# Gathered expert rows transposed as f32r, with a comparison against fp32 transposes for the first expert

## The chip, the cores and the metric

The kernel runs on one core of one Trainium2 chip. The metric is the device time of one execution, in microseconds (us). The core's engines are TensorE (PE in the profile, with PEld for its weight loads), VectorE (DVE), ScalarE (ACT), GpSimd (POOL) and SyncE (SP), which issues most of the DMAs. Each engine works through a queue of its own in order; semaphores tie the queues together.

## The reference

Two blocks of a model run one after the other on x of 1024 tokens by 1024 features. The first block is a mixer (attention with latent queries and keys, and a chunked recurrent branch) followed by a mixture of experts; the second is two layers of a mixer with four branches. The change lies in the mixture of experts. Each of the 16 experts takes the 128 tokens that have the highest affinity to it:

```python
def ec_moe(x, w_router, w_e_gate, w_e_up, w_e_down):
    B, T, D = x.shape
    cap = CAP_FACTOR * T // N_EXPERTS                  # 128
    aff = jax.nn.softmax((x @ w_router).astype(jnp.float32), axis=-1)
    g, idx = lax.top_k(aff.transpose(0, 2, 1), cap)
    xs = jax.vmap(lambda xb, ib: xb[ib])(x, idx)
    a = jnp.einsum('becd,edf->becf', xs, w_e_gate)
    u = jnp.einsum('becd,edf->becf', xs, w_e_up)
    y = jnp.einsum('becf,efd->becd', jax.nn.silu(a) * u, w_e_down) * g[..., None].astype(x.dtype)
    return jax.vmap(lambda yb, ib: jnp.zeros((T, D), x.dtype).at[ib.reshape(-1)].add(yb.reshape(-1, D)))(y, idx)
```

All of it is fp32; one expert has three weight matrices of 1024 by 1024.

## The kernel before

A product in fp32 accuracy is made of three passes over operands of type f32r (a 32-bit type with fewer bits of mantissa): each operand is split into a high half H, which ScalarE writes by a copy that rounds to f32r (L141), and a low half L, which VectorE makes as the difference (L142). The passes are H by H, L by H and H by L.

The expert stage begins near 1480 us and goes to 2096 us of the span. For expert e:

- `slots(e)` finds the 128 token numbers. VectorE makes eight one-hot tiles `hot` (L1197, 16 buffers), TensorE multiplies each by `pick` and sums into a PSUM tile named "tp" (L1198; each of the eight products is two instructions, 16 in all), and VectorE copies the result to `idxT` (L1199) and to `gsl` (L1200), which holds the gate weights g.
- `tokens(e)` gathers the rows from DRAM with an indirect DMA that POOL issues (L1207), into `xs`, two buffers deep.
- `transposed(xs, "xT")` turns the rows: two times four transposes of 128x128 on TensorE against an identity (L1162), each four into one PSUM tile "tp", which is then split into xTH and xTL. There are two "tp" buffers, shared by `slots`, by the transposes of the rows and by those of the hidden activations ("eT").
- `product(xT, w)` loads the weights in four tiles of 1 MB (twelve tiles deep in all, named ewr and ahead), splits them into ewH and ewL of 128x1024, four buffers of each, and for each of eight k makes six multiplications of 128x512 into `acc` (L1188): ewH by xTH and ewH by xTL for the two halves of the columns, then ewL by xTH.
- The gate product goes through Silu on ScalarE to `ea` (L1212), VectorE multiplies the up product into it (L1231), the result is transposed ("eT") and goes through the down product; VectorE scales it by `gsl[:, e]` (L1237), and POOL adds the rows to the output with a scattering DMA (L1238).

The loop is written so that the transposes for expert e + 1 and the slots of expert e + 2 stand ahead of the up product of expert e. That isn't the order on the chip: a scheduler orders each engine's instructions when the program is built, by its own estimate of the times, so a change at one place can shift instructions elsewhere. The two layers of the second block follow the expert stage; the attention jobs in them (one head by 256 queries each, 20 in the first layer, four of them short, and 16 in the second) are ordered in the same way. `ident` is an fp32 identity, `identr` (L153) the same in f32r, which other transposes use already (L838).

Of the kernel before, what the change touches and what calls it, by code (L numbers as in the profile page):

```python
# [10 lines left out]
F32 = mybir.dt.float32  # L11
F32R = mybir.dt.float32r
U32 = mybir.dt.uint32
I32 = mybir.dt.int32
AF = mybir.ActivationFunctionType
OP = mybir.AluOpType
AX = mybir.AxisListType
# [3 lines left out]
P = 128  # L21
D = 1024
# [100 lines left out]
def build(ctx, tc, A, out):  # L123
# [6 lines left out]
    V, S, G, PE, SY = nc.vector, nc.scalar, nc.gpsimd, nc.tensor, nc.sync  # L130
# [21 lines left out]
    ident = load(const, A["k_ident"], [P, P], "ident")  # L152
    identr = const.tile([P, P], F32R, name="identr")  # L153
# [250 lines left out]
    with ExitStack() as es:  # L404
# [4 lines left out]
        for j in range(4):  # L409
# [3 lines left out]
                               op0=OP.add, op1=OP.mult)  # L413
    with ExitStack() as es:
# [4 lines left out]
        ps = es.enter_context(tile_pool(name="ps1", bufs=1, space=PSUM))  # L419
# [36 lines left out]
        with ExitStack() as es2:  # L456
            tp = es2.enter_context(tile_pool(name="gw", bufs=1, side="right", reuse_waits="tile"))
            bd = block_diagonals(tp, load(tp, A["k_blk"], [P, P], "blk"))
            wg = load(tp, A["w_gate"][0].rearrange("(f p) g -> p f g", p=P), [P, 24, 16], "wg")
            for f in range(8):  # L460
                pt = ps.tile([P, 512], F32, name="gw", bufs=1)
# [15 lines left out]
        for f2 in range(4):  # L477
            wt = wstream(wp, win, 704 + 256 * f2)
            for f in (2 * f2, 2 * f2 + 1):
# [13 lines left out]
                for a, b in ((0, C), (C, N)):  # L493
                    for j in (0, 1, 3, 4):
# [3 lines left out]
                                               op0=OP.mult, op1=OP.add)  # L498
# [75 lines left out]
    with ExitStack() as es:  # L574
        gp = es.enter_context(tile_pool(name="mg", bufs=1, reuse_waits="tile"))
        ps = es.enter_context(tile_pool(name="ps2", bufs=1, space=PSUM))
# [48 lines left out]
        for d, st_ in ((0, 1), (1, -1)):  # L625
            r = DIR[d]
            V.tensor_tensor_scan(Bc[r, ::st_], ones[r, ::st_], LF[r, ::st_], 0.0, op0=OP.mult, op1=OP.add)
        V.tensor_sub(Aa, IG, Bc)
        for d, st_ in ((0, 1), (1, -1)):
            r = DIR[d]  # L630
# [6 lines left out]
        pr = psc()  # L637
# [4 lines left out]
        for h in range(4):  # L642
            f0, b0 = 10 * h, 64 + 10 * h
            V.tensor_tensor_scan(R[:, 2, f0:f0 + 10], R[:, 0, f0:f0 + 10], R[:, 1, f0:f0 + 10], 0.0,
                                 op0=OP.max, op1=OP.add)
# [27 lines left out]
        pt = psc()  # L673
# [475 lines left out]
    with ExitStack() as es:  # L1149
# [6 lines left out]
        def transposed(src, nm):  # L1156
            H = tp.tile([P, 8, P], F32R, name=nm + "H")
            L = tp.tile([P, 8, P], F32R, name=nm + "L")
            for hb in range(2):
                pt = ps.tile([P, 512], F32, name="tp", tag="tp", bufs=2)  # L1160
                for j in range(4):
                    PE.transpose(pt[:, j * P:(j + 1) * P], src[:, (4 * hb + j) * P:(4 * hb + j + 1) * P], ident)  # L1162
                hs_ = slice(4 * hb, 4 * hb + 4)
                split(H[:, hs_].rearrange("p a b -> p (a b)"), L[:, hs_].rearrange("p a b -> p (a b)"), pt)
            return H, L
# [37 lines left out]
        at = lambda e: bass.IndirectOffsetOnAxis(ap=idxT[:, e:e + 1], axis=0)  # L1203

        def tokens(e):
            xs = sp.tile([P, D], F32, name="xs")
            G.indirect_dma_start(out=xs, out_offset=None, in_=h2_scr, in_offset=at(e))  # L1207
            return xs

        def gated(xT, e):  # L1210
# [6 lines left out]
        xs = tokens(0)  # L1217
        slots(1)
        xT = transposed(xs, "xT")
        xs = tokens(1)  # L1220
        with tc.issue_after(chosen.ins):
            a = gated(xT, 0)
# [513 lines left out]
```

## Time and profile before

| | before |
|---|---|
| median of 3 runs | 3334.95 us (3334.73 to 3339.39) |
| the profiled execution | 3336.31 us |
| its span | 3334.5 us |
| mean granted TensorE clock over the span | 0.972 |
| TensorE busy | 3142.5 us, 94% |
| VectorE busy | 2239.7 us, 67% |
| ScalarE busy | 1551.2 us, 47% |
| GpSimd busy | 662.8 us, 20% |

The profile is of one execution, the one with the span in the table. Its views are a page (busy times, slices, the costliest groups), tables by stretch of time, a list of what an engine waited for, and the timeline of one engine. A row of a timeline gives the start, the duration, engine, line and operation, the tiles (out, then in), the shapes, the number of instructions taken together, and in brackets the idle time before and what ended it. In every view a multiplication's record begins when it enters the pipeline, and its end is modelled, so records of TensorE overlap; the distance from one start to the next is what it costs. A granted clock of 1.00 is 2.4 GHz and one of 0.50 is 1.2 GHz.

### The profile page before, as it was taken

What the parts mean: (1) busy time and instruction counts of PE and PEld (TensorE: products, weight loads), DVE (VectorE), ACT (ScalarE), POOL (GpSimd) and SP (SyncE); (2) the same over time, 40 slices, a digit from 0 to 9 for tenths busy, and PEclk for the clock granted to TensorE, in tenths of its full rate; (3) what the DMA queues carried; (4) which work ended last, traced back from release to release, by engine and by line L of the source; (5) the groups of instructions that cost most, each with busy time, mean ns of one, the idle gap of its engine ahead of it and who ended that gap; (6) DMA issues with size and microseconds to landing.
All of it is one profiled execution on the core that took longest, in us unless ns stands there. A gap on an engine that the chain in (4) does not pass through costs nothing. (4 is left out here: it accounts for less than half of the span.)

```text
span 3334.5 us, 48219 instructions
## 1 busy us (share of the span) xinstructions
PE 3142.5 (94%) x17297; PEld 2650.8 (79%) x17297; DVE 2239.7 (67%) x4868; ACT 1551.2 (47%) x3076; POOL 662.8 (20%) x840
## 2 busy tenths in 40 slices
PE   7997998999999999969999999799999998999999
PEld 5885886999998888857888877698877887887787
DVE  4485778767666654498999888777527745642783
ACT  4223444555555222217777767621126824312780
POOL 0012232222222000331121100210114601101450
PEclk9998999999999999979999999899999999999999
DMA  8541112000003532458999998433210033111002
GB/s 295 147 124 36 36 43 65 5 15 10 5 11 104 153 112 64 169 201 319 380 367 386 366 336 303 149 100 108 67 39 32 1 128 127 51 48 50 32 27 101
DMA packets 224011, 425.95 MB, mean 128 GB/s; under 512 B 28684, under 2 KB 121468, under 8 KB 223772
## 3 DMA queue, kind: packets, MB, share of 16 engines
q1 hardware_dynamic: 215708, 393.51, 33.5%
q0 software_dynamic: 8064, 29.36, 3.0%
q8 instruction: 136, 2.23, 0.3%
q14 instruction: 103, 0.84, 0.1%
HBM read 379.22 MB, written 43.61 MB: 127 GB/s over the span
## 5 line engine op out<-in xcount | busy, mean ns | idle before, releaser
L145 PE MATMUL acc<-hH,wHL 128*128 128x512 f32 (+1 forms) x1296 | 485.4, 376 | 5.5 <-ACT wHL L141 3.9
L146 PE MATMUL acc<-hL,wHL 128*128 128x512 f32 (+1 forms) x1296 | 484.1, 374 | 0.0
L147 PE MATMUL acc<-hH,wHL 128*128 128x512 f32 (+1 forms) x1296 | 482.4, 373 | 0.0
L142 DVE TENSOR_TENSOR ewL<-ewr,ewH 128x1024 fp32r<-128x1024 f32 x320 | 377.9, 1220 | 37.1 <-ACT ewH L141 27.7
L141 ACT ACTIVATE ewH<-ewr 128x1024 fp32r<-128x1024 f32 x320 | 335.9, 1061 | 121.9 <-PE acc L1188 116.0
L145 PEld LDWEIGHTS acc<-hH,wHL 128*128 128x128 f32 x1296 | 244.5, 189 | 53.9 <-ACT wHL L141 6.7
L146 PEld LDWEIGHTS acc<-hL,wHL 128*128 128x128 f32 x1296 | 244.6, 189 | 44.5 <-issue 2.6
L147 PEld LDWEIGHTS acc<-hH,wHL 128*128 128x128 f32 x1296 | 244.2, 189 | 44.4 <-issue 1.6
L142 DVE TENSOR_TENSOR wHL<-wr,wHL 128x512 fp32r<-128x512 f32 (+1 forms) x160 | 111.8, 703 | 222.9 <-ACT wHL L141 222.5
L142 DVE TENSOR_TENSOR et<-t,et 128x512 fp32r<-128x512 f32 x264 | 179.6, 685 | 58.6 <-ACT et L141 57.1
L141 ACT ACTIVATE et<-t 128x512 fp32r<-128x512 f32 x264 | 156.3, 605 | 133.6 <-PE t L904 111.7
L141 ACT ACTIVATE wHL<-wr 128x512 fp32r<-128x512 f32 (+1 forms) x160 | 101.8, 639 | 247.5 <-PE acc L146 221.1
L1188 PE MATMUL acc<-ewH,xTL 128*128 128x512 f32 x512 | 203.5, 397 | 2.3 <-DVE xTL L142 2.3
L1188 PE MATMUL acc<-ewH,xTH 128*128 128x512 f32 x512 | 204.4, 399 | 1.1 <-ACT xTH L141 1.1
L302 DVE SCALAR_TENSOR_TENSOR ga<-gw,lh,ga 128x512 f32<-128x512 f32 x224 | 161.1, 747 | 51.0 <-DMA gw<-in_w_mod_dram 49.4
L183 POOL TENSOR_SCALAR E<-E,sm 128x512 f32<-128x512 f32 (+1 forms) x192 | 117.9, 633 | 326.8 <-ACT E L172 106.6
L1188 PE MATMUL acc<-ewL,xTH 128*128 128x512 f32 x512 | 162.5, 401 | 0.0
L170 DVE TENSOR_REDUCE sm<-s 128x1 f32<-128x512 f32 (+1 forms) x192 | 113.2, 598 | 60.4 <-PE s L888 55.6
L145 PE MATMUL acc<-wHL,hH 128*128 128x256 f32 (+1 forms) x464 | 143.3, 317 | 3.3 <-DVE hH L1282 2.1
L146 PE MATMUL acc<-wHL,hH 128*128 128x256 f32 (+1 forms) x464 | 138.5, 304 | 0.0
L1564 DVE TENSOR_REDUCE mx<-s 128x1 f32<-128x512 f32 (+1 forms) x200 | 114.8, 588 | 28.3 <-PE s L1563 26.3
L147 PE MATMUL acc<-wHL,hL 128*128 128x256 f32 (+1 forms) x464 | 129.5, 314 | 4.4 <-DVE hL L1283 4.0
(545 smaller groups left out, 7958.6 us busy)
## 6 DMA issues: line engine op xcount, KB each, us to landing
ewr<-in_w_e_up_dram SPq DMA_DIRECT2D x64, 1024.0 KB
ewr<-in_w_e_gate_dram SPq DMA_DIRECT2D x62, 1024.0 KB
wr<-in_w_in_dram SPq DMA_DIRECT2D x152, 256.0 KB
ewr<-in_w_e_down_dram SPq DMA_DIRECT2D x34, 1024.0 KB
ahead<-in_w_e_down_dram SPq DMA_DIRECT2D x30, 1024.0 KB
gw<-in_w_mod_dram SPq DMA_DIRECT2D x96, 256.0 KB
gw<-in_w_mod_dram SPq DMA_DIRECT2D x32, 512.0 KB
wm<-in_w_mod_dram SPq DMA_DIRECT2D x4, 2048.0 KB
```

Of the source, the lines that this page charges most:

```text
L141: S.activation(H, src, AF.Copy)
L142: V.tensor_sub(L, src, H)
L145: PE.matmul(o, lh[0], rh[0], start=start, stop=False)
L146: PE.matmul(o, lh[0], rh[1], start=False, stop=False)
L147: PE.matmul(o, lh[1], rh[0], start=False, stop=stop)
L170: V.tensor_reduce(ng[:, b:b + 1], sc, axis=AX.X, op=OP.max)
L183: G.tensor_scalar(E[:, k0:k0 + n], E[:, k0:k0 + n], f[:, b:b + 1], 1.0, op0=OP.mult, op1=OP.mult)
L302: V.scalar_tensor_tensor(acc[x], wk, ck, acc[x], op0=OP.mult, op1=OP.add) if k else
L1188: PE.matmul(pa[:, n], x[:, k], w[:, 512 * n:512 * n + 512], start=k == 0 and x is xT[0] and w is H, stop=k == 7 and w is L)
L1564: V.tensor_reduce(mx[:, b:b + 1], sc[:, :n], axis=AX.X, op=OP.max)
```

## The change

The gathered rows now land in a tile of type f32r (the DMA writes them through an fp32 view, so the bits are the same), and the eight transposes of "xT" run as f32r, with `identr` and into a PSUM tile of type f32r that is read as fp32. The transposes of "eT" stay fp32. For the first expert alone, a comparison is added: for each of the eight blocks of 128 columns, TensorE transposes the rows once as fp32 (po) and once as f32r (pr), each into a "tp" tile of its own; ScalarE copies the fp32 result to a tile `hot`, VectorE compares the two (not_equal) and reduces the row to its maximum. The sum of the eight, times 1000, is added to expert 0's gate weights, so they change only where the two transposes differ.

```diff
@@ -1157,9 +1157,12 @@
             for hb in range(2):
-                pt = ps.tile([P, 512], F32, name="tp", tag="tp", bufs=2)
+
+                r = nm == "xT"
+                pt = ps.tile([P, 512], F32R if r else F32, name="tp", tag="tp", bufs=2)
                 for j in range(4):
-                    PE.transpose(pt[:, j * P:(j + 1) * P], src[:, (4 * hb + j) * P:(4 * hb + j + 1) * P], ident)
+                    PE.transpose(pt[:, j * P:(j + 1) * P], src[:, (4 * hb + j) * P:(4 * hb + j + 1) * P], identr if r else ident)
+                pt = pt.bitcast(F32) if r else pt
@@ -1203,8 +1206,8 @@
         def tokens(e):
-            xs = sp.tile([P, D], F32, name="xs")
-            G.indirect_dma_start(out=xs, out_offset=None, in_=h2_scr, in_offset=at(e))
+            xs = sp.tile([P, D], F32R, name="xs")
+            G.indirect_dma_start(out=xs.bitcast(F32), out_offset=None, in_=h2_scr, in_offset=at(e))
@@ -1217,6 +1220,19 @@
         xT = transposed(xs, "xT")
+
+        bad = sp.tile([P, P], F32, name="hot", bufs=16)
+        for k in range(8):
+            po = ps.tile([P, 512], F32, name="tp", tag="tp", bufs=2)
+            PE.transpose(po[:, :P], xs.bitcast(F32)[:, k * P:(k + 1) * P], ident)
+            pr = ps.tile([P, 512], F32R, name="tp", tag="tp", bufs=2)
+            PE.transpose(pr[:, :P], xs[:, k * P:(k + 1) * P], identr)
+            sm_ = sp.tile([P, P], F32, name="hot", bufs=16)
+            S.activation(sm_, po[:, :P], AF.Copy)
+            V.tensor_tensor(sm_, sm_, pr[:, :P].bitcast(F32), op=OP.not_equal)
+            V.tensor_reduce(bad[:, k:k + 1], sm_, axis=AX.X, op=OP.max)
+        V.tensor_reduce(bad[:, 8:9], bad[:, 0:8], axis=AX.X, op=OP.add)
+        V.scalar_tensor_tensor(gsl[:, 0:1], bad[:, 8:9], 1000.0, gsl[:, 0:1], op0=OP.mult, op1=OP.add)
         xs = tokens(1)
```

In the changed kernel the lines behind the first hunk stand three further down, and those of the main loop sixteen: L1162 becomes L1164, L1188 becomes L1191, the one-hot sums L1198 become L1201, L1197 becomes L1200, and the multiplication of ea, L1231, becomes L1247. New are the fp32 transposes of the comparison L1227, its f32r transposes L1229, the not_equal L1232 and the reductions L1233.

The scheduler then orders some places in another way. First, TensorE's queue at the turn from expert 0 to expert 1. Before, the last multiplications of expert 0's up product (into acc_14877) go over into the gate product of expert 1 (into acc_14968, with the rows xTH_14832 and xTL_14833):

```order
L1188 MATMUL acc_14877<-ewH_14956,xTL_14728 128x512
L1188 MATMUL acc_14968<-ewH_14971,xTH_14832 128x512
L1188 MATMUL acc_14877<-ewL_14957,xTH_14727 128x512 x2
L1188 MATMUL acc_14968<-ewH_14971,xTL_14833 128x512
L1188 MATMUL acc_14968<-ewH_14971,xTH_14832 128x512
L1188 MATMUL acc_14968<-ewH_14971,xTL_14833 128x512
```

In the changed order the up product's last two multiplications stand first here, and the gate product of expert 1 goes into acc_15035:

```order
L1191 MATMUL acc_14944<-ewL_15024,xTH_14727 128x512 x2
L1229 MATMUL tp_14778<-identr_70,xs_14698 128x128
L1227 MATMUL tp_14784<-ident_68,xs_14698 128x128
L1229 MATMUL tp_14786<-identr_70,xs_14698 128x128
L1227 MATMUL tp_14792<-ident_68,xs_14698 128x128
L1229 MATMUL tp_14794<-identr_70,xs_14698 128x128
L1227 MATMUL tp_14800<-ident_68,xs_14698 128x128
L1229 MATMUL tp_14802<-identr_70,xs_14698 128x128
L1164 MATMUL tp_14901<-identr_70,xs_14810 128x128 x4
L1191 MATMUL acc_15035<-ewH_15038,xTH_14899 128x512
L1164 MATMUL tp_14908<-identr_70,xs_14810 128x128 x4
L1201 MATMUL tp_14915<-pick_11642,hot_14916 128x2
```

Between the two products stand now seven of the comparison's transposes, the eight transposes of expert 1's rows and, behind the first multiplication, the one-hot sums of expert 2, of which the last row is the first of sixteen.

VectorE's queue at the same place. Before, around the multiplication of ea for expert 0:

```order
L142 TENSOR_TENSOR ewL<-ewr,ewH 128x1024 x6
L1231 TENSOR_TENSOR ea<-acc,ea 128x1024
L142 TENSOR_TENSOR ewL<-ewr,ewH 128x1024 x5
L142 TENSOR_TENSOR eTL<-tp,eTH 128x512 x2
L142 TENSOR_TENSOR ewL<-ahead,ewH 128x1024 x4
L142 TENSOR_TENSOR ewL<-ewr,ewH 128x1024
L142 TENSOR_TENSOR xTL<-tp,xTH 128x512 x2
```

In the changed order, from the multiplication of ea for expert 0 to the first xTL of expert 1:

```order
L1247 TENSOR_TENSOR ea<-acc,ea 128x1024
L1232 TENSOR_TENSOR hot<-hot,tp 128x128
L142 TENSOR_TENSOR ewL<-ewr,ewH 128x1024
L1232 TENSOR_TENSOR hot<-hot,tp 128x128
L1233 TENSOR_REDUCE hot<-hot 128x1
L1232 TENSOR_TENSOR hot<-hot,tp 128x128
L1233 TENSOR_REDUCE hot<-hot 128x1
L1200 TENSOR_SCALAR hot<-ktop,codeT 128x128 x2
L1233 TENSOR_REDUCE hot<-hot 128x1
L1200 TENSOR_SCALAR hot<-ktop,codeT 128x128 x3
L1232 TENSOR_TENSOR hot<-hot,tp 128x128
L1200 TENSOR_SCALAR hot<-ktop,codeT 128x128 x9
```

The row behind these is the first xTL of expert 1; four comparisons, three reductions and fourteen one-hots now stand between ea and it.

VectorE's queue at the start of the stage. Before, from the last step of the routing on:

```order
L1146 COPY codeT<-p_14652 128x128
L1197 TENSOR_SCALAR hot<-ktop,codeT 128x128 x23
L1199 CAST idxT<-tp 128x1
L1200 COPY gsl<-tp 128x1
L142 TENSOR_TENSOR ewL<-ahead,ewH 128x1024 x4
L1197 TENSOR_SCALAR hot<-ktop,codeT 128x128 x8
L1199 CAST idxT<-tp 128x1
```

In the changed order:

```order
L1146 COPY codeT<-p_14652 128x128
L1200 TENSOR_SCALAR hot<-ktop,codeT 128x128 x16
L1202 CAST idxT<-tp 128x1
L1203 COPY gsl<-tp 128x1
L142 TENSOR_TENSOR ewL<-ahead,ewH 128x1024 x4
L1202 CAST idxT<-tp 128x1
L1203 COPY gsl<-tp 128x1
```

The first index column has now sixteen one-hots ahead of it instead of 23; the one-hots of expert 2 went from here to the turn above.

## Rows read from the trace of the kernel before

**Rows 1.** The page, busy time of each engine, share of the span and instructions.

```profile
PE 3142.5 (94%) x17297; PEld 2650.8 (79%) x17297; DVE 2239.7 (67%) x4868; ACT 1551.2 (47%) x3076; POOL 662.8 (20%) x840
```

**Rows 2.** Table by stretches: one expert, and 3.6 us later on; columns stand first.

```profile
core 0: us, PE busy (x) PEld busy (x) DVE busy (x) ACT busy (x) POOL busy (x), PEclk, DMA share, GB/s
1560.00:1597.00 37.00, 37.00 (x181) 31.05 (x180) 34.99 (x43) 28.41 (x30) 6.67 (x3) 1.00 0.99 376
...
1899.10:1902.70 3.60, 3.60 (x11) 2.82 (x11) 3.60 (x12) 1.06 (x1) 0.86 (x1) 0.56 1.03 381
```

**Rows 3.** Waits of TensorE, 1505 to 2096 us: us in total, times, longest.

```profile
PE tp L1198 <- DVE xTL L142: 5.6, 3, 2.3
PE acc L1188 <- DVE xTL L142: 2.3, 1, 2.3
```

**Rows 4.** Timeline of TensorE between two experts, 1894 to 1903 us.

```profile
1894.11 1.03 PE L1162 MATMUL tp<-ident,xs 128*128 128x128 f32 x8
1895.39 0.49 PE L1188 MATMUL acc<-ewH,xTH 128*128 128x512 f32 x1 [0.25 <-ACT xTH L141]
1897.32 1.95 PE L1198 MATMUL tp<-pick,hot 128*128 128x2 f32 x16 [1.43 <-DVE xTL L142]
1899.12 0.48 PE L1188 MATMUL acc<-ewH,xTL 128*128 128x512 f32 x1
...
1902.31 0.63 PE L1188 MATMUL acc<-ewH,xTL 128*128 128x512 f32 x1
1902.74 0.74 PE L1188 MATMUL acc<-ewL,xTH 128*128 128x512 f32 x2
```

**Rows 5.** Timeline of VectorE at the same place.

```profile
1894.30 1.22 DVE L1231 TENSOR_TENSOR ea<-acc,ea 128x1024 f32<-128x1024 f32 x1 [1.65 <-PE acc L1188]
1895.44 1.22 DVE L142 TENSOR_TENSOR ewL<-ewr,ewH 128x1024 fp32r<-128x1024 f32 x1
1896.58 1.28 DVE L142 TENSOR_TENSOR xTL<-tp,xTH 128x512 fp32r<-128x512 f32 x2
```

**Rows 6.** Timeline of TensorE, eight fp32 transposes between multiplications of 128x512.

```profile
1546.47 1.03 PE L1162 MATMUL tp<-ident,xs 128*128 128x128 f32 x8
1547.27 0.71 PE L1188 MATMUL acc<-ewL,eTH 128*128 128x512 f32 x2
1547.81 0.39 PE L1188 MATMUL acc<-ewH,eTH 128*128 128x512 f32 x1
```

**Rows 7.** Timeline of TensorE, four f32r transposes between multiplications of 128x256.

```profile
842.69 0.46 PE L838 MATMUL t<-identr,et 128*128 128x128 f32 x4
842.98 0.35 PE L147 MATMUL s<-wv,kvT 128*128 128x256 f32 x1
843.17 0.28 PE L145 MATMUL s<-wv,kvT 128*128 128x256 f32 x1
843.28 0.28 PE L146 MATMUL s<-wv,kvT 128*128 128x256 f32 x1
```

**Rows 8.** VectorE's instructions by line: busy us, mean ns, idle before.

```profile
L1114 DVE TENSOR_REDUCE th<-best 16x1 f32<-16x128 f32 x1 | 0.3, 274 | 0.0
```

**Rows 9.** Timeline of all engines at the start of the expert stage.

```profile
1489.94 4.59 DVE L1197 TENSOR_SCALAR hot<-ktop,codeT 128x128 f32<-128x128 f32 x23
...
1490.37 6.96 PE L1198 MATMUL tp<-pick,hot 128*128 128x2 f32 x32 [0.86 <-DVE hot L1197]
...
1494.45 0.15 DVE L1199 CAST idxT<-tp 128x1 uint32<-128x1 f32 x1
...
1505.73 1.94 PE L1162 MATMUL tp<-ident,xs 128*128 128x128 f32 x8 [8.40 <-DMA xs<-h_scr,idxT]
```

**Rows 10.** Table by stretches: those one-hot sums, attention of both layers; columns as above.

```profile
1490.00:1497.00 7.00, 6.63 (x32) 6.66 (x32) 7.00 (x28) 3.59 (x4) 1.55 (x1) 0.50 0.15 57
2516.70:2671.50 154.80, 139.32 (x963) 122.42 (x961) 122.26 (x360) 120.86 (x317) 84.54 (x119) 0.97 0.05 19
3101.70:3239.90 138.20, 129.40 (x899) 114.17 (x897) 111.05 (x307) 113.38 (x294) 78.71 (x107) 0.95 0.04 13
```

## The prediction, made before the changed kernel had run

> **What bounds the kernel now.** I read the page first: TensorE is busy for 94% of the span, no other engine for more than 67% [rows 1]. Then the table by stretches: over one expert of the expert stage TensorE is busy for all of the 37.0 us at its full clock, VectorE for 34.99 us, ScalarE for 28.41 us [rows 2]. So the stage goes at TensorE's pace, VectorE has some 2 us to spare per expert, and what is added to TensorE's queue or makes it wait moves the end; the DMA, at a share of 0.99, still has its tiles ready: TensorE waits for none of them after the start.
>
> Then the waits of TensorE in the stage. Four times it waited for xTL, the low half of the transposed rows [rows 3]. I call this a late turn: the eight transposes of the next expert's rows stand directly ahead of the first multiplication that needs them. One is shown in [rows 4]. From the first transpose at 1894.11 to the row at 1902.74 pass 8.63 us. The work in it takes, at the stage's own rates, 0.89 (eight transposes) + 1.80 (the sixteen instructions of the one-hot sums, 1897.32 to 1899.12) + 2.27 (ten multiplications at 0.227) = 4.96 us. So a late turn loses 3.7 us. Two parts: some 2.1 us of waiting, and 1.6 us because nine multiplications behind it start up to 0.43 us apart instead of 0.227: after the engine had idled, the granted clock is 0.56 from 1899.10 to 1902.70 [rows 2], mostly at the lower of its two levels, 1.2 instead of 2.4 GHz. VectorE's rows show why it waited: when the product ends, VectorE first multiplies ea, then makes one ewL, then the two xTL [rows 5]. Its queue is served in order.
>
> **The change part by part.** *Transposes as f32r.* Eight fp32 transposes between multiplications take 0.80 us to the next start, and that start is followed by another 0.54 us for two instead of 0.45: 0.89 us, 0.11 each [rows 6]. Four f32r transposes elsewhere take 0.29 us and then 0.19 instead of 0.12: 0.36 us, 0.09 each [rows 7]. There are 128 of them on the bounding engine: 128 x 0.02 = 2.7 us gained. Bounds: nothing, where VectorE ends a wait anyway, and 3.2 us by the rounding.
>
> Here a rule differs from the rows. The Trainium skill (FP8 and Floating Point Precision, TensorE Precision Notes) counts four passes through the array for true fp32 and one for reduced precision. By it an f32r transpose would cost a quarter of 0.11, 0.03 us; the rows do not agree, with 0.09 beside 0.11. By that rule this term would be 10.5 us; I keep it as a rival.
>
> *The comparison on TensorE.* Eight fp32 and eight f32r transposes of 128 columns: 8 x 0.11 + 8 x 0.09 = 1.6 us added. Eight of ScalarE's copies hide in its 8 us to spare.
>
> *The comparison on VectorE, and the new wait.* No row shows not_equal on PSUM. From 128x1024 at 1.14 us [rows 5] and 128x512 at 0.64 a column costs about 1 ns; I put 0.28 us for 128 columns, an estimate; a reduction of 128 columns takes 0.27 [rows 8]. For k = 0 to 3 these stand among ewL's in the loosely filled start and I cost them at nothing beyond the transposes. For k = 4 to 7 they do not hide. The order shows seven comparison transposes, the eight of expert 1's rows, one multiplication and the one-hot sums of expert 2 all packed between the end of expert 0's up product and the second multiplication of expert 1's gate product. Only two "tp" buffers serve them, so each waits until a copy or a not_equal has emptied one. And VectorE stands like this between that end and the first xTL: ea 1.14, ewL 1.14, four not_equal 1.12, three reductions 0.81, fourteen one-hots at 4.59 / 23 = 0.20 [rows 9] 2.80, xTL 0.68: 7.7 us in a row. It begins about 0.2 us after the product's end, as at 1894.30 [rows 5]. TensorE goes on with the one-hot sums at 7.9 us and with multiplications at 9.7 us, or at 11.3 us if the clock has fallen by then (32 such instructions took 6.96 us [rows 9], at a granted clock of 0.50 [rows 10], so sixteen take 3.45). Of that 0.7 (comparison, counted above) + 0.7 + 0.23 + 1.8 = 3.4 us is work that has to be done in any case. Loss: 6.3 to 7.9 us, and up to 1.6 us of half clock behind it, as in [rows 4]: 6.3 to 9.5. I take 8.7, near the upper end: TensorE is nearly idle for longer than in [rows 4], where the clock fell. A bound from below is a late turn's 3.7 us. Before, there was no wait at this turn. Nothing gives the loss back later: the weights are there anyway, and TensorE is the bound.
>
> *The start.* Before, 23 one-hots stand ahead of the first index column, though sixteen instructions of PE end at about 1490.37 + 3.45 = 1493.8; the column came at 1494.45 [rows 9]. With sixteen it comes some 0.4 us sooner, and so does the gather, for which TensorE waits until 1505.73. The one-hots that were made in this shadow are now part of the 7.7 us. I take 0.5 us gained with slightly faster transposes at half clock; bounds 0 and 1.
>
> *Late turns elsewhere.* In the changed order the transposes of the next rows stand directly ahead of their use at experts 10, 11, 12 and 14 instead of 11, 12, 13 and 15: four as before. At one of them one ewL more stands ahead of xTL (1.1 us). I put 0.5 us lost, bounds 1.5 us on either side.
>
> *The second block.* No instruction changes, but the order in the attention does, in some six jobs of layer 0 and nearly all sixteen of layer 1. The two stretches already differ in order, and cost 138.2 us for 16 jobs, and 154.8 us for those 16 and 4 short ones [rows 10], so one order is about as good as another: 0, bounds 2.5 us on either side.
>
> Sum: -2.7 + 1.6 + 8.7 - 0.5 + 0.5 = +7.6 us. The profiled execution has a span of 3334.5 us and took 3336.31 us; with +7.6 that is 3343.9. The median of the runs shown, 3334.95, is 1.4 us below it, so I forecast 3342.5 us. About 0.2%, or 6.7 us, is what a measurement can tell from no change: the forecast is just beyond it.
>
> **The rivals.**
> 1. *A short turn.* The new wait is no worse than a late turn of [rows 4], 3.7 us, because VectorE gets through its small instructions while TensorE still works (they come ready one by one, and if TensorE lags VectorE by some 4 us at that point, half of the 7.7 us lie beside multiplications). For it: [rows 5] show VectorE idle-free there only for a moment. Against it: ea needs the whole product. -2.7 + 1.6 + 3.7 - 0.5 + 0.5 = +2.6: 3337.5 us, no change.
> 2. *Not slower: f32r transposes at one pass.* By the rule above 128 x 0.08 = 10.5 us are gained and the comparison costs 1.1 us. -10.5 + 1.1 + 8.7 - 0.5 + 0.5 = -0.7: 3334 us. It decides from 0.09 us each downwards: below about 0.05 the new wait is paid for. Against it speak the 64 transposes of which [rows 7] show four.
> 3. *The change does not do what it says.* The f32r transposes of gathered rows cost as much as the fp32 ones, since the weight load ahead of them sets the pace. Then 2.7 us fall away: 3345.5 us.
> 4. *More late turns, or a bad order in the attention*: 3.7 us for one more, 2.5 us for the attention: 3349 us.
>
> **How the numbers follow.** The forecast has 0.54 (its own range 3338.5 to 3346), rival 1 0.23, rival 2 0.08, rival 3 0.07, rival 4 0.08. From the forecast and rivals 3 and 4 come 0.52 of slower; from the forecast's lower end, rival 1 and half of rival 2 0.43 of no change; 0.05 of faster. The range of 3335.5 to 3348 takes in rival 1 and most of rival 4.
>
> **What would show it right or wrong.** In the changed profile: a wait of TensorE for xTL at the turn to expert 1, near 1531 us, with 8 to 10 us from the last multiplication of the up product to the second of the gate product, and a granted clock below 1.0 right behind it. Blocks of eight f32r transposes at 0.70 us. Four late turns. The attention of both layers within 2.5 us of before. The forecast is wrong if the new turn takes under 7 us, if the f32r block takes 0.3 us or 0.9, or if the stages behind 2110 us move by more than the expert stage.

## The result, and the profile after

The changed kernel took 3360.23 us (median of four runs, 3358.9 to 3363.7) beside 3334.84 us of the kernel before. The ratio is 1.0062, with a 95% interval of 1.0047 to 1.0077: 20.7 us slower, 15.7 to 25.7. The medians by themselves lie 25.4 us apart, a ratio of 1.0076; how the recorded 1.0062 comes from these eight executions can't be seen. A second comparison on another chip, with all its executions on record, gave 1.0062 again (1.0049 to 1.0075), and the sums below go by that ratio. The forecast was 7.6 us slower, at most 13: the direction is right, the size is not, and the time lies above the range. The kernel before has medians of 3334.8 to 3341.9 us from chip to chip, so ratios are compared below; 0.001 is 3.3 us. One of the twelve executions of cmp_spread, a run below, took 9127.9 us and stands in no ratio.

The page of the changed kernel shows the same division of work as [rows 1], with a span of 3361.9 us (its execution took 3363.7):

```profile
PE 3163.0 (94%) x17313; PEld 2664.1 (79%) x17313; DVE 2243.3 (67%) x4886; ACT 1552.5 (46%) x3084; POOL 655.5 (19%) x840
```

TensorE's waits in the expert stage, as in [rows 3] (us in total, times, longest):

```profile
PE tp L1201 <- DVE xTL L142: 9.2, 5, 2.5
PE acc L1191 <- ACT xTH L141: 2.7, 6, 0.7
...
PE tp L1227 <- DVE hot L1232: 1.7, 2, 1.5
PE tp L1229 <- ACT hot L1231: 1.0, 2, 0.7
```

The waits for xTL were 7.9 us in four places and are 9.2 us in five: the fifth is the turn to expert 1. The two last rows are the comparison waiting for its two tp buffers.

**The turn to expert 1** looks as forecast. TensorE's timeline there (start, duration, instruction, idle time and what ended it):

```profile
1529.52 0.63 PE L1191 MATMUL acc<-ewL,xTH 128*128 128x512 f32 x2
...
1532.73 0.33 PE L1227 MATMUL tp<-ident,xs 128*128 128x128 f32 x1 [1.46 <-DVE hot L1232]
...
1536.34 0.79 PE L1191 MATMUL acc<-ewH,xTH 128*128 128x512 f32 x1 [0.69 <-ACT xTH L141]
1536.93 0.67 PE L1164 MATMUL tp<-identr,xs 128*128 128x128 f32 x4
1538.38 3.57 PE L1201 MATMUL tp<-pick,hot 128*128 128x2 f32 x16 [0.78 <-DVE xTL L142]
1541.82 0.77 PE L1191 MATMUL acc<-ewH,xTL 128*128 128x512 f32 x1
...
1546.65 0.61 PE L1191 MATMUL acc<-ewH,xTH 128*128 128x512 f32 x1
```

and VectorE's:

```profile
1530.14 1.21 DVE L142 TENSOR_TENSOR ewL<-ewr,ewH 128x1024 fp32r<-128x1024 f32 x1
1531.27 1.21 DVE L1247 TENSOR_TENSOR ea<-acc,ea 128x1024 f32<-128x1024 f32 x1
...
1535.88 1.84 DVE L1200 TENSOR_SCALAR hot<-ktop,codeT 128x128 f32<-128x128 f32 x9
1537.65 0.68 DVE L142 TENSOR_TENSOR xTL<-tp,xTH 128x512 fp32r<-128x512 f32 x1
```

The up product ends at about 1530.0 and its successor's second multiplication starts at 1541.82: 11.8 us, where the prediction's working had 11.3 with the clock down (and its list of signs 8 to 10). VectorE goes from ea to xTL in one row of work, 1531.27 to 1538.3, 7.0 us where 7.7 were summed; it started 1 us late, since an ewL stood ahead of ea. One-hot sums take 3.57 us, at half clock.

**The late turns** are four again, as forecast, but they cost more. The one at expert 11, on TensorE and on VectorE:

```profile
1908.76 0.79 PE L1164 MATMUL tp<-identr,xs 128*128 128x128 f32 x8
1910.10 0.50 PE L1191 MATMUL acc<-ewH,xTH 128*128 128x512 f32 x1 [0.55 <-ACT xTH L141]
1913.11 3.57 PE L1201 MATMUL tp<-pick,hot 128*128 128x2 f32 x16 [2.51 <-DVE xTL L142]
```

```profile
1908.96 1.23 DVE L1247 TENSOR_TENSOR ea<-acc,ea 128x1024 f32<-128x1024 f32 x1 [0.75 <-PE acc L1191]
1910.10 2.35 DVE L142 TENSOR_TENSOR ewL<-ewr,ewH 128x1024 fp32r<-128x1024 f32 x2
1912.37 1.28 DVE L142 TENSOR_TENSOR xTL<-tp,xTH 128x512 fp32r<-128x512 f32 x2
```

Against [rows 4, 5] there is one ewL more ahead of xTL (forecast), and the one-hot sums run at half clock at once, 3.57 us instead of 1.95. The granted clock (third number from the end; the columns are those of [rows 2]) behind three of the late turns of after, and behind two of before:

```profile
1913.10:1922.60 9.50, 9.49 (x30) 8.20 (x31) 4.94 (x13) 2.11 (x2) 0.97 (x1) 0.50 0.81 320
1956.90:1963.60 6.70, 6.66 (x24) 6.01 (x25) 3.41 (x12) 1.06 (x1) 0.97 (x1) 0.50 1.01 402
2035.50:2042.00 6.50, 6.43 (x23) 5.88 (x24) 1.02 (x4) 1.06 (x1) 0.97 (x1) 0.50 1.03 414
```

```profile
1937.90:1943.90 6.00, 6.00 (x28) 5.09 (x29) 3.62 (x12) 1.71 (x2) 0.97 (x1) 0.72 1.03 417
1979.10:1984.90 5.80, 5.80 (x27) 4.93 (x28) 1.89 (x4) 1.37 (x2) 0.97 (x1) 0.71 1.02 412
```

Read: from the end of the wait on, TensorE is busy in all of them; in after it has half its speed (1.2 instead of 2.4 GHz) for all of these 6.5 to 9.5 us, in before for the later part of some 6 us: 0.72 on the mean over 6.0 us is 3.4 us at half speed.

**The second layer's attention**, against the last row of [rows 10]:

```profile
3125.80:3267.30 141.50, 130.44 (x899) 113.97 (x897) 110.83 (x307) 112.59 (x294) 78.86 (x107) 0.97 0.04 12
```

The same 899 instructions take 141.5 instead of 138.2 us, at a clock that is no lower.

### The profile page after: what moved, and what is told of

It is laid out like the page before. It is cut to its first block, busy times and chain, and to the rows that moved or that the text cites. A ratio compares the mean times of both kernels' runs of the same rounds, so it can differ in the third digit from the quotient of the medians.

```text
span 3361.9 us, 48290 instructions
## 1 busy us (share of the span) xinstructions
PE 3163.0 (94%) x17313; PEld 2664.1 (79%) x17313; DVE 2243.3 (67%) x4886; ACT 1552.5 (46%) x3084; POOL 655.5 (19%) x840
## 4 chain that ended last, share of the span: by engine, by line
PE 80%; DVE 9%; ACT 3%; DMA 3%; issue 2%; POOL 1%; SPq 0%; ACTq 0%; POOLq 0%; DVEq 0%
PE acc L1191 15%; PE acc L145 11%; PE acc L146 11%; PE acc L147 11%; PE s L145 2%; PE s L147 2%; PE s L146 2%; PE t L904 2%; PE o L1621 2%; PE s L1579 2%; PE u L763 2%; PE t L1605 1%; PE ni L744 1%; PE o L146 1%; PE s L888 1%
## 5 line engine op out<-in xcount | busy, mean ns | idle before, releaser
L1191 PE MATMUL acc<-ewH,xTH 128*128 128x512 f32 x512 | 207.2, 405 | 2.7 <-ACT xTH L141 2.7
L1191 PE MATMUL acc<-ewH,xTL 128*128 128x512 f32 x512 | 206.3, 403 | 0.0
L1191 PE MATMUL acc<-ewL,xTH 128*128 128x512 f32 x512 | 163.9, 404 | 0.0
L1254 POOL DMA_INDIRECT acc_scr<-ey,idxT x16 | 55.3, 3458 | 413.3 <-DVE ey L1253 274.0
```

The source lines that it names most:

```text
L1191: PE.matmul(pa[:, n], x[:, k], w[:, 512 * n:512 * n + 512], start=k == 0 and x is xT[0] and w is H, stop=k == 7 and w is L)
```

## The experiments

Because a scheduler orders the program anew after each edit, most kernels here have their queues forced: a table holds the number of every instruction, engine by engine, and each is tied to the one ahead of it in the table (order only, no wait). The edit is this, with some lines left out, and below only the source of the table is said:

```diff
+def ordered(tc):
+    by = {i.name: i for i in tc.nc.cur_bb.bb.instructions}
+    dep = mybir.DependencyInfo(mybir.DependencyClass.NoSync, mybir.DependencyReason.DATA)
+    for steps in json.loads(zlib.decompress(base64.b85decode("".join(_ORDER)))):
+        last = at = None
+        for d in steps:
+            at = d if at is None else at + d
+            i = by.get(f"I-{at}")
...
+            if last is not None:
+                tc.add_manual_dep(i, last.name, dep, reason="order")
+            last = i
...
             build(ctx, tc, aps, out)
+            ordered(tc)
```

Two stretches are compared over all traces, by the starts of rows: the expert stage, from the first one-hot sum to the last multiplication of the last down product (1490.4 to 2106.3 us in before, where the 2096 us given above fall ten short), and the second layer's attention, from its first scores to its last values. With the ratio to the kernel before on the same chip (a name with _2 is a second comparison of the same kernel):

```
kernel                   ratio (95%)             stage us       2nd attention us
before                                           615.9, 616.1   138.0, 137.8
after                    1.0062 (1.0047-1.0077)  629.0          141.3
after_again              1.0062 (1.0049-1.0075)  622.9          141.3
f32r_border              1.0003 (0.9994-1.0011)  616.6          137.9
fp32_aorder              1.0060 (1.0047-1.0073)  628.4          141.4
f32r_only                1.0028 (1.0018-1.0038)  620.1          137.8
before_attn              1.0026 (1.0017-1.0035)  620.4          141.2
after_battn              1.0040 (1.0025-1.0056)  627.0          138.0
cmp_spread               0.9996 (0.9987-1.0004)  615.9          138.2
f32r_periodic            0.9937 (0.9923-0.9951)  598.4          137.9
fp32_periodic            0.9940 (0.9926-0.9954)  602.1          138.1
cmp_periodic, _2         0.9944, 0.9938          596.4, 594.5   138.1, 138.0
cmp_per_attn             0.9944 (0.9928-0.9959)  594.3          142.5
after_periodic, _2       0.9986, 0.9979          602.8, 603.7   141.8, 142.8
```

### Are the f32r transposes the cause? (f32r_border, fp32_aorder, f32r_only)

My first theory after the result was that f32r transposes let the clock fall sooner at a late turn than fp32 ones (A); its rival was that the changed order does it (B). f32r_only is the change without the comparison; f32r_border is that kernel in before's order:

```diff
-        bad = sp.tile([P, P], F32, name="hot", bufs=16)
-        for k in range(8):
...
-        V.scalar_tensor_tensor(gsl[:, 0:1], bad[:, 8:9], 1000.0, gsl[:, 0:1], op0=OP.mult, op1=OP.add)
```

fp32_aorder is the changed kernel in its own order, with fp32 transposes:

```diff
         def transposed(src, nm):
+            src = src.bitcast(F32) if nm == "xT" else src
...
-                r = nm == "xT"
+                r = False
```

> Rows land in f32r and are transposed as f32r, no comparison, and every engine's queue stands in exactly the order of the kernel before (forced). Theory A (the clock): in the changed kernel's four late turns the sixteen one-hot instructions took 2.57 to 3.57 us instead of 1.92 to 1.95, because the granted clock fell there sooner than behind fp32 transposes. Then f32r transposes lose about 2 us at each of the four late turns and gain 2.7 us over the rest: 3340 us, +5. Theory B (the order): f32r transposes only gain, by 0.02 us each, and the longer late turns came from the changed order: 3332 us, -2.7.

> The changed kernel with its comparison and in exactly its order (forced), but the rows of the sixteen experts are transposed as fp32 for use. Theory A: the late turns are shorter by 2 us each and the one-hot sums there take 1.95 us again, the 128 transposes cost 2.7 us more: 3355 us, 5 below the changed kernel. Theory B: 2.7 us above the changed kernel, 3363, and the one-hot sums at the late turns still take about 3.5 us.

> The change without the comparison, in the scheduler's own order, which has three late turns with nothing between the last transpose and the use, one with two multiplications between and two with eight. Without the comparison the wait of 8.7 us at the turn to expert 1 and 1.6 us of transposes go. Theory A: six more or less late turns at up to 6 us each, 3345 to 3350 us. Theory B: 3335 to 3340 us.

Measured: 1.0003, 1.0060 and 1.0028. In the changed order, fp32 transposes take as long as f32r ones (1.0060 and 1.0062); in before's order f32r changes nothing that can be measured. A in its stated size, 5 us either way, does not show in the ratios, and B's plain gain of 2.7 us doesn't either: in f32r_border the interval is 2 us faster to 4 us slower. In fp32_aorder the one-hot sums of the four late turns took 1.95, 3.57, 2.35 and 2.87 us, neither A's 1.95 nor B's 3.5. The median of f32r_only, 3345.77 us, lies in the range of A; but it has six waits for xTL of 0.4 to 2.5 us, in an order of its own, and cannot tell order from type.

The clock behind a wait differs between executions of one program. The same turn in three traces shows that: in fp32_aorder and in after the one-hot sums behind the wait of 2.51 us run at half clock, in after_again, the same kernel as after with the same wait there, they do not.

```profile
1907.47 3.57 PE L1202 MATMUL tp<-pick,hot 128*128 128x2 f32 x16 [2.51 <-DVE xTL L142]
```

```profile
1909.27 1.95 PE L1201 MATMUL tp<-pick,hot 128*128 128x2 f32 x16 [2.51 <-DVE xTL L142]
```

The first is of fp32_aorder, the second of after_again. So neither type nor order alone decides how soon the clock falls. That f32r transposes have some part in it is not excluded: priced as under the late turns in the account of the prediction below, the four of them lose 17.7, 17.7 and 20.7 us in the three traces with fp32 and before's order, 21.0 and 21.3 with f32r in that order, 22.9 with fp32 in after's order, and 22.0, 25.7 and 26.3 with f32r in it. By these few traces f32r gives back at the late turns some 2 us of what it gains, and the order costs some 4; neither is clear of the spread between executions.

### What the late turns cost, and what a transpose costs (f32r_periodic, fp32_periodic)

In before, experts 1 to 5 have one and the same order, with the transposes 90 multiplications ahead of their use. Here that of expert 3 is repeated for experts 4 to 15 (table: before's, with those numbers rearranged).

> f32r transposes without comparison; all queues as in the kernel before, except that experts 4 to 15 repeat the order of expert 3 in it, in which the transposes stand 90 multiplications ahead of their use (forced). If the late turns are a matter of the order alone, the 21 us that the four of them lost with f32r transposes go: 3316 us, and TensorE waits for no xTL in the stage. If they are there because rows or weights come late, other waits take their place: 3330 us or more.

> The kernel before with fp32 transposes and that same repeated order. Without late turns nothing depends on how long VectorE lets TensorE wait, so against the f32r one this gives the price of the transposes alone: 128 x 0.02 = 2.7 us more, 3319 us. If f32r takes one pass of four, 10.5 us more; if it costs the same, 3316.

Measured: 0.9937 and 0.9940; that is 3319.60 and 3322.74 us where before took 3341.92. TensorE's waits of f32r_periodic from 1500 us to the end of the stage, all of them:

```profile
PE tp L1164 <- DMA xs<-h_scr,idxT: 8.4, 1, 8.4
PE acc L1191 <- ACT ewH L141: 1.7, 1, 1.7
PE tp L1164 <- DVE ea L1235: 1.3, 1, 1.3
PE acc L1191 <- ACT xTH L141: 0.2, 1, 0.2
```

No wait for xTL is left; the one for ewH, 1.7 us at the last expert, is new, and nothing else took their place: the late turns are a matter of the order. By fp32_periodic they cost the kernel before 0.0060, 20 us. And a transpose can be read here undisturbed, eight f32r ones in f32r_periodic:

```profile
1654.60 0.79 PE L1164 MATMUL tp<-identr,xs 128*128 128x128 f32 x8
1655.23 0.69 PE L1191 MATMUL acc<-ewL,eTH 128*128 128x512 f32 x2
1655.76 0.39 PE L1191 MATMUL acc<-ewH,eTH 128*128 128x512 f32 x1
```

0.63 us to the next start, and 0.08 more behind that: 0.71 us, as forecast, against 0.89 in [rows 6]. Sixteen times 0.18 is 2.9 us. The stage is 3.7 us shorter, of which 1.4 lie at the start (16.8 and 15.4 us from the first one-hot sum to the first transposes) and 2.3 behind it; the median is 3.1 us lower, which the intervals of the two ratios do not tell from nothing. The Trainium skill (FP8 and Floating Point Precision, TensorE Precision Notes) gives true fp32 four passes through the array; it says so of precision, not of transposes. Had f32r transposes needed a quarter of that, the gain would by the prediction's estimate be 10.5 us; 0.71 beside 0.89 us does not agree with that for transposes.

### What the comparison costs (cmp_spread, cmp_periodic, after_periodic)

cmp_spread has the whole change, in before's order, with the comparison's eight steps placed one by one in expert 0's gate product. cmp_periodic is the same with the repeated order. after_periodic keeps the changed kernel's own order up to expert 3, with the turn, and has the repeated order behind.

> f32r transposes, the order of the kernel before (forced), and the whole comparison, but its eight steps stand one by one behind every fourth of the first 30 multiplications of expert 0's gate product, on TensorE, ScalarE and VectorE; the one-hots of experts 2 and 3 that stood ahead of that are behind it. If the comparison costs by the wait at the turn to expert 1: its own 1.6 us on TensorE and some tenths for each change of the two tp buffers, so 2 to 4 us over the same kernel without it (3336.9): 3339 to 3341 us. If it costs wherever it stands (buffers, VectorE): 7 to 9 us, 3344 to 3346.

> The whole change (f32r transposes and comparison), with the comparison spread over expert 0's gate product, experts 4 to 15 in the repeated order, and the second block in the order of before (forced). If the comparison is free where VectorE has room: 0.9937 to 0.9945 of before, about 3320 us and 20 us faster than before. If it costs 7 us wherever it stands: 0.996.

> The changed kernel with its own order at the turn to expert 1 and in the second block, but experts 4 to 15 in the repeated order without late turns (forced). If the loss of the change is the turn to expert 1 (7 us by the traces), the late turns made dearer, and the second layer's attention (3.3 us): the late turns go, and what stays over the f32r kernel in the repeated order (0.9937 of before) is 10 us: 0.9967. If comparison and turn cost little: 0.994 to 0.995; if the comparison also slows later stages: 0.999 or more.

Measured: 0.9996, 0.9944 and 0.9986. So spread out, the whole change costs nothing that can be measured: cmp_spread is as fast as before and as f32r_border. Two things work against each other in it. The comparison's own work costs some us (the stage of cmp_periodic, cmp_periodic_2 and cmp_per_attn is 3.3 us shorter on the mean than that of f32r_periodic, while their start is 5.9 us shorter: 2.6 us). And the start gained more than I had seen. The gather of expert 0's rows, on POOL, in before:

```profile
1495.44 4.68 POOL L1207 DMA_INDIRECT xs<-h_scr,idxT  x1 [31.58 <-DVE gsl L1200]
```

and in after, with the index column ahead of it and the transposes that wait for it:

```profile
1497.34 0.16 DVE L1202 CAST idxT<-tp 128x1 uint32<-128x1 f32 x1 [0.79 <-PE tp L1201]
...
1498.34 1.27 POOL L1210 DMA_INDIRECT xs<-h_scr,idxT  x1 [31.08 <-DVE gsl L1203]
...
1503.25 1.23 PE L1164 MATMUL tp<-identr,xs 128*128 128x128 f32 x8 [2.54 <-DMA xs<-h_scr,idxT]
```

From the first one-hot sum, 1493.76, to these transposes pass 9.5 us; by [rows 9] it was 15.4. Of these 5.9 us the column brings 0.5 (3.6 instead of 4.1 us behind the first one-hot sum), POOL 3.4, and from POOL's end to the transposes it is 2.0 us less. All ten traces with sixteen one-hots ahead of the gather have 9.3 to 9.6 us and POOL at 1.27 or 1.28, and all seven with 23 have 15.3 to 16.8 and 4.68.

At the turn, the same work costs 8.2 us more than spread out: stages of 602.8 and 603.7 us in after_periodic against 596.4, 594.5 and 594.3 in the three with the comparison spread.

### The second block's order (before_attn, after_battn), and what chance does (after_again, before_again)

before_attn is before with the second block's queues of after; after_battn the reverse.

> The kernel before, with the two layers of the second block in the changed kernel's order (forced), and the expert stage as before. Theory C (the attention's order costs): in the two profiles the changed kernel loses 1.5 us in the attention of the first layer and 4.8 us in that of the second, so 3340 to 3341 us. Theory D (one order is as good as another): within 2 us of before, and the profile shows the second layer's attention at 138.2 +- 2 us.

> The changed kernel as it is, with its own order up to the end of the expert stage, and the two layers of the second block in the order of the kernel before (forced). If the order of the attention is part of the loss: between 3.3 us (what the second layer's attention, 141.2 to 141.4 instead of 137.8 to 138.0 us, shows in the traces) and 8.6 us (the difference of the times of the kernel before with that order alone) below the changed kernel, 3351.5 to 3357 us. If the attention's order is not: 3360 us.

> The changed kernel once more, beside the kernel before on one chip. Its first profile was 3.4, 5.1 and 2.5 us longer in three stretches whose instructions and order are those of before (up to the first one-hot sums, between the expert stage and the first attention, between the two attentions), with more half clock in them. If that is chance of one execution: these stretches come back to within 2 us of before, and the ratio lies near 1.0045 (12 us in the expert stage and 3.3 in the second attention). If the change causes it: 1.006 to 1.008 again, and the same stretches long again.

> The kernel before once more, one look, for a second trace of it: the same stretches within 2 us of the first trace (1490.4, 615.9, 410.5, 154.6, 430.4, 138.0 and 94.7 us) if a trace can be read to that; 3 to 5 us off in some of them if the granted clock falls by chance in unchanged code.

Measured: 1.0026 and 1.0040, 8.7 us from before (5.7 to 11.7) and 7.3 from after; the 7.3 compares two chips, and the intervals of the two ratios overlap. The rows of the second layer's attention, before_attn first:

```profile
3103.90:3245.20 141.30, 130.67 (x898) 114.31 (x897) 110.85 (x307) 112.38 (x294) 78.80 (x107) 0.95 0.04 12
```

```profile
3114.30:3252.30 138.00, 129.05 (x897) 113.76 (x897) 110.85 (x307) 113.53 (x294) 78.58 (x107) 0.97 0.04 13
```

The attention's length goes with its order, 137.8 to 138.2 us in the ten traces with before's or f32r_only's, 141.2 to 142.8 in the seven with after's. Where it goes can be read from the first and last starts of the scores and the values, of before and of after:

```profile
L1563 PE MATMUL s<-kst,qst x192: 278/393/795, 3101.8 to 3227.0; 128*128 128x512 f32 x128, 128*128 128x256 f32 x64
```

```profile
L1605 PE MATMUL o<-et,vst x320: 274/283/388, 3116.3 to 3239.8; 128*128 128x256 f32 x160
```

```profile
L1579 PE MATMUL s<-kst,qst x192: 276/393/796, 3125.9 to 3247.6; 128*128 128x512 f32 x128, 128*128 128x256 f32 x64
```

```profile
L1621 PE MATMUL o<-et,vst x320: 274/283/386, 3139.9 to 3267.2; 128*128 128x256 f32 x160
```

In the changed order the scores are done 3.5 us sooner (121.7 after 125.2 us), but 19.6 us of values stand behind the last score instead of 12.8: the scores ran ahead, and the end has less to fill the waits with. The end of the attention in before and in after:

```profile
3220.00:3240.00 20.00, 18.91 (x135) 15.91 (x133) 14.10 (x36) 13.83 (x34) 10.78 (x14) 1.00 0.00 1
```

```profile
3247.60:3267.30 19.70, 16.93 (x127) 14.62 (x125) 10.96 (x25) 11.70 (x27) 10.46 (x13) 1.00 0.00 1
```

TensorE idles for 1.1 and 2.8 us in them, which is half of the 3.4 us; where the other half goes is not shown.

The attention is 3.4 us of the 7 to 9. Of the rest, 4.4 us lie in before_attn's trace in the expert stage (620.4 us), whose order is before's: two of its late turns had the longer half clock. after_again's profiled execution took 3355.53 us and before_again's 3338.07. Of the three unchanged stretches that were long in the first trace of after, the one up to the first one-hots came back (1491.7 us, 1491.1 in before_again); those behind the stage and between the attentions are still 3.2 and 2.8 us longer than in before_again. For one of them there is a place: near 2370 us VectorE waits for gw, a weight of the second block, ahead of what TensorE needs. In after:

```profile
2368.26 1.41 DVE L302 SCALAR_TENSOR_TENSOR ga<-gw,lh,ga 128x512 f32<-128x512 f32 x2 [0.78 <-DMA gw<-in_w_mod_dram]
2370.98 1.42 DVE L302 SCALAR_TENSOR_TENSOR ga<-gw,lh,ga 128x512 f32<-128x512 f32 x2 [1.31 <-DMA gw<-in_w_mod_dram]
```

The second of these waits is not there in before. From one multiplication to the next pass there 2.9 and 3.4 us in the two traces of after, 1.7 and 1.9 in those of before, and in after the clock falls behind it. From the stage to the first attention pass 411.0 to 415.6 us in the four traces with after's order of all experts and 406.5 to 412.5 in the five with before's, so this too is not clear of chance.

### The price of the order and of the turn, by times (cmp_per_attn, cmp_periodic_2, after_periodic_2)

These three ran on one chip; cmp_per_attn is cmp_periodic with the second block in after's order, so it differs from after_periodic_2 in the start, the turn and the two experts behind it alone.

> The whole change with the comparison spread over expert 0's gate product and the repeated order for experts 4 to 15 (as cmp_periodic), but the second block in the changed kernel's order (forced). There are no late turns here, so the clock has fewer chances to fall in the stage. If the attention's order costs what the traces show: 3.4 us over cmp_periodic_2 of the same call. If it costs what the times of two kernels with that order alone differ by: 7 to 9 us.

> The same as cmp_periodic, once more, as the reference of this call: 0.9944 of before again (0.993 to 0.996).

> The same as after_periodic, once more: it differs from cmp_per_attn only in the changed kernel's own start and turn to expert 1 and the two experts behind it. By the traces (602.8 and 596.4 us for the stage) 6.4 us over cmp_per_attn; by the times 14 us over cmp_periodic_2, of which the attention's order takes its part.

Measured: 3323.27, 3320.79 and 3333.31 us. Where no late turns are, the second block's order costs 2.5 us by times (0.9944 and 0.9938), and the turn, with the start and the two experts behind it, 10.0 us. Both agree with the traces, but the ratios' intervals leave some 7 us on either side of each, so the times alone show only that the turn costs something.

## Why the prediction fell short, step by step

- **The new wait** (8.7 us, range 6.3 to 9.5) was right: 8.2 us by the stages, 10.0 by the times, though from product to product it took 11.8 us where the list of signs had 8 to 10. Rival 1, a short turn of 3.7 us, falls.
- **The f32r transposes** (2.7 us gained) were right as a price: 0.71 us for eight, 2.9 us in all, and 2.3 us by the stages where no late turn stands. Whether the changed kernel keeps all of it at its late turns is not shown. Rivals 2 and 3 fall (3345.5 us in rival 3 should read 3345.2).
- **The comparison's work** (1.6 us) was mis-sized a little: about 2.6 us. What it adds beyond its transposes are waits for the tp buffers.
- **The start** (0.5 us gained, bounds 0 and 1) was mis-sized: 5.9 us gained. I had reckoned with the index column alone, and that came 0.5 us sooner as forecast; 3.4 us are the gather's time on POOL, which fell from 4.68 to 1.27 us, and 2.0 the way from there to the transposes.
- **The late turns** (0.5 us lost, bounds 1.5 us either side) is the step that failed. With each multiplication at 0.227 us and each one-hot sum instruction at 0.1125, as in the prediction, and a transpose at 0.111 or 0.088, the four turns lose 17.7 us in both traces of before and 26.3 and 22.0 in those of after, 4 to 9 us more. By times, after loses 0.0076 to 0.0083 to after_periodic, 25 to 28 us, and before 0.0060 to fp32_periodic, 20 us: 5 to 8 us more, with some 7 us of interval on either side. I had counted turns and VectorE's instructions, and both were right; I had not counted that what follows a wait may run at half clock for 6.5 to 9.5 us (at three of the four in the first trace) instead of 3.4, with 1.8 us of one-hot sums behind each of the four instead of three. Rival 4 had a fifth turn for such a size, not four dearer ones; its other half, the attention at 2.5 us, came true.
- **The second block** (0, bounds 2.5 us) failed too. That two layers with different orders took similar times said nothing of a third order: the second layer's attention is 3.4 us longer, beyond the 2.5 us that were the sign of being wrong.
- Behind the stage I expected nothing; the wait for gw with the clock's fall adds 2.6 and 4.3 us in the two traces, a size that chance also has there. In after_again the stages behind the stage of the experts moved more than that stage, some 10 and 6.8 us against before_again, which the prediction had named as a sign of being wrong.

Together: 8.2 - 2.9 + 2.6 - 5.9 + (4 to 9) + 3.4 + (2.6 to 4.3) = 12 to 19 us, with 20.7 measured and 15.7 the low end of its interval. Open stays whether the second block's order costs more than its attention shows (before_attn and after_battn move by 7 to 9 us, the attention by 3.4 and cmp_per_attn by 2 to 2.5, all with wide intervals), and why the clock falls at once behind some waits and later behind others of the same length; that the changed order has more of the early falls is seen in four of its traces (22.0 to 26.3 us lost at the late turns) beside five with before's order there (17.7 to 21.3), and is not explained; the transposes' type may have a part in it.

The best version is a by-product: the repeated order alone, at 0.9940 with fp32 and 0.9937 with f32r transposes, 20 and 21 us faster than before; even the whole change with its comparison spread is at 0.9938 to 0.9944.

## What to carry to other kernels

When a scheduler orders the program, an edit is also a new order, and the order can cost more than the edit: force the old order on the new instructions, and the new order on the old ones, before a cause is sought in the instructions. A short stop of the bounding engine is worth its length and the half clock behind it; count both, with the second as a range. Work that compares or checks should stand where a neighbour has room, not in one row ahead of what the bound engine waits for: the same eight steps cost some 2.6 us spread out and 8.2 us more in a row.

## What was not expected of the hardware

The first gather on POOL took 4.68 us in all seven traces with 23 one-hots ahead of it and 1.27 or 1.28 in all ten with sixteen, with four ewL of VectorE in a row in each, of which the first begins 0.85 us before the gather in before and 0.86 in after; later gathers in before take 0.96 us where VectorE pauses and 5.06 where its ewL follow one another. The Trainium skill (SBUF — State Buffer, Who interferes with whom) says that a VectorE instruction with two SBUF inputs, as ewL has, stands against a GpSimd instruction that reads SBUF; the 5.06 and the 0.96 us agree with it, the 1.27 beside two ewL does not by itself, nor do four later gathers of 1.7 us beside ewL in after, and no run here explains the two values. That the gather is truly shorter shows in TensorE's wait for it, 2.54 instead of 8.40 us. And one program, with the same waits of 2.51 us, ran the sixteen instructions behind them in 3.57 us in one execution and in 1.95 in another.
